# Summing the second layer's modulation vectors on VectorE instead of TensorE

## The chip, the cores and the metric

The kernel runs on one core of one Trainium2 chip. What counts is the device time of one execution in microseconds (us). The five engines of the core (PE = TensorE, DVE = VectorE, ACT = ScalarE, POOL = GpSimd, SP, which here only issues DMAs) each run their own list of instructions in order and wait for each other by semaphores.

## The reference, cut to what matters

The program is a transformer block with dilated attention, followed by two layers that are modulated by a conditioning vector. Everything is fp32. The part that the change touches is the modulation of the second layer (i = 1):

```python
def modulation(cvec, w, b):
    m = jax.nn.silu(cvec) @ w + b              # (1024,) @ (1024, 6144)
    return jnp.split(m[..., None, :], 6, axis=-1)

for i in range(2):
    sh1, sc1, g1, sh2, sc2, g2 = modulation(c, w_mod[i], b_mod[i])
    csh1, csc1, cg1, csh2, csc2, cg2 = modulation(c_ctx, w_mod[i], b_mod[i])
    h = x * (1.0 + sc1) + sh1
    hc = xc * (1.0 + csc1) + csh1
    ...                                        # mixer of the layer
    x = layer_norm(alpha * x + g1 * y)
    x = layer_norm(alpha * x + g2 * mlp(x * (1 + sc2) + sh2))   # mlp: relu(h @ w1)**2 @ w2
```

Each weight matrix w_mod[i] is 1024 x 6144 fp32, 25.2 MB, and it is read for two vectors (c and c_ctx). In the last layer the context stream needs only sh1 and sc1, so four of the six slices are needed for one vector alone.

## The kernel before, in words

The tokens are 256 of the stream and 256 of the context, in four tiles T of 128 tokens (T = 0, 1 context; T = 2, 3 stream). Large products are done in three fp32r products each: a weight tile of 128 x 1024 (`raw`, 512 KB) is loaded by SP, ScalarE rounds it to `whi` (line 134), VectorE makes the remainder `wlo` (line 135), and TensorE adds hi*hi, hi*lo and lo*hi (`mm3`, lines 158 to 160).

The first layer's MLP (`mlp`) runs over eight groups g of 512 hidden units. In each group the first product (w1) makes four hidden column tiles; ScalarE takes the relu (line 1002), VectorE squares (`f`, line 1003), ScalarE and VectorE split the result into `fx` (lines 110 and 111); then the second product (w2) is added to `y` by VectorE (lines 1012 and 1014). In g = 0 the w1 product is done in two parts, first for the context tokens, then for the stream, because the modulated input `hB` of the tiles comes one by one from `modulate`: TensorE transposes the normalised rows r (line 194), ScalarE applies scale and shift (`hf`, line 302), VectorE splits into `hBh` and `hBl` (lines 304 and 305). At the same time GpSimd computes the new residual streams (`new_resid`, lines 955 and 956: eight operations of 128 x 1024).

The second layer's modulation is computed during this MLP by three generators `quad` in the list `fillers`. Each covers 2048 columns; in 8 steps k it loads two pieces `mvraw` of 128 x 1024 (512 KB, three buffers, line 246) and multiplies them on TensorE by `cst_m[:, k, :]`, the two conditioning vectors padded to 32 columns (line 240): four products of 512 columns in fp32, one for each group of 32 output partitions, into the PSUM bank "O". The result is copied with the bias on VectorE (line 256), transposed into columns by `to_cols` (line 194 and 272), or written to DRAM for later row broadcasts. `fill(rate[0])` advances a generator by so many steps whenever a weight tile is requested (`w_a`, `w_b`); rate is 2 in the MLP.

The order on each engine is decided when the program is built, by a scheduler with a timeline model (`schedule_with_timeline_sim=True`), so code that is written later can stand earlier on its engine.

Of the kernel before, what the change touches and what calls it, by code (L numbers as in the profile page):

```python
# [10 lines left out]
F32 = mybir.dt.float32  # L11
# [3 lines left out]
ALU = mybir.AluOpType  # L15
# [80 lines left out]
def body(tc, a, cst, out):  # L96
    nc = tc.nc
    with ExitStack() as ctx:
        const = ctx.enter_context(tc.tile_pool(name="const", bufs=1))
        wpool = ctx.enter_context(tc.tile_pool(name="wpool", bufs=5))  # L100
        small = ctx.enter_context(tc.tile_pool(name="small", bufs=6))
        dram = ctx.enter_context(tc.tile_pool(name="dram", bufs=1, space=DRAM))
# [3 lines left out]
        def bank(tag):  # L106
            return psum.tile([P, 512], F32, tag=tag, name=tag, bufs={"mm": 3, "S": 2, "T": 2, "O": 1}[tag])
# [5 lines left out]
        fillers = []  # L113
# [12 lines left out]
        rate = [0]  # L126
# [81 lines left out]
        cst_m = const.tile([P, KC, 32], F32, tag="cst_m", name="cst_m")  # L208
        nc.gpsimd.memset(cst_a, 0.0)
        nc.gpsimd.memset(cst_m, 0.0)  # L210
        nc.gpsimd.memset(neghalf, -0.5)
        nc.vector.tensor_copy(cst_a[:, :, 0], cv[:, 2, :])
        make_identity(nc, ident)
        xs = const.tile([P, 2, D], F32, tag="xs", name="xs")
# [7 lines left out]
        b1 = ctx.enter_context(ExitStack())  # L222
        p1t = b1.enter_context(tc.tile_pool(name="p1t", bufs=2))

        def quad(pool, rpool, key, w, col, b, stat, vecs, n=512, rows=""):


            bias = pool.tile([P, n], F32, tag="mvb", name="mvb", bufs=1)
            nc.gpsimd.memset(bias, 0.0)
            for m in range(vecs):  # L230
                nc.gpsimd.dma_start(bias[m::32, :], b[col:col + 4 * n].rearrange("(j n) -> j n", n=n))
            acc = bank("O")
            wv = w.rearrange("(p k) n -> p k n", k=KC)
            todo = []

            def product():
                k, raws_ = todo.pop(0)
                for j in range(4):
                    raw = raws_[j * n // 1024]
                    nc.tensor.matmul(acc[32 * j:32 * j + 32, :n], stat[:, k, :], raw[:, j * n % 1024:j * n % 1024 + n], start=k == 0, stop=k == KC - 1)  # L240

            for k in range(KC):
                raws_ = []
                for h in range(n // 256):
                    raw = pool.tile([P, 1024], F32, tag="mvraw", name="mvraw", bufs=3)
                    nc.sync.dma_start(raw, wv[:, k, col + 1024 * h:col + 1024 * h + 1024])
                    raws_.append(raw)
                    yield
                todo.append((k, raws_))
                if len(todo) > 0:  # L250
                    product()
            while todo:
                product()
                yield
            r = rpool.tile([P, n], F32, tag="R" + key, name="R" + key, bufs=1) if rpool else tmp([P, n], "R" + key)
            nc.vector.tensor_add(r, acc[:, :n], bias)
            R[key] = r
            if rows:
                rd = dram.tile([vecs, 4 * n], F32, tag="rd" + rows, name="rd" + rows)
                for m in range(vecs):  # L260
                    nc.gpsimd.dma_start(rd[m].rearrange("(j n) -> j n", n=n), r[m::32, :])
                RD[rows] = rd
            yield

        def to_cols(r, name, tag="T"):

            pt = bank(tag)
            n = r.shape[-1] // P
            for c in range(n):
                transpose(pt[:, c * P:(c + 1) * P], r[:, c * P:(c + 1) * P])  # L270
            cols = const.tile([P, 4, n, 2], F32, tag=name, name=name)
            nc.vector.tensor_copy(cols, pt[:, :n * P].rearrange("p (c j r) -> p j c r", j=4, r=32)[:, :, :, 0:2])
            return cols.rearrange("p j c m -> p (j c) m")

        def to_rows(g, key, vec, at):

            nc.gpsimd.dma_start(g, bcast_rows(RD[key][vec, at:at + D]))
# [168 lines left out]
        def quad0():
            yield from quad(p1t, None, "0", w_mod[0], 0, b_mod[0], cst_m, 2)
            m0["a"] = to_cols(R["0"], "m0a")

        fillers.append(quad0())  # L450
        fillers.append(quad(p1t, const, "b", w_mod[0], 2048, b_mod[0], cst_m, 2, rows="b0"))
        fillers.append(quad(p1t, const, "c", w_mod[0], 4096, b_mod[0], cst_m, 2, rows="c0"))
        rate[0] = 2

        qT, kT = [], []
# [126 lines left out]

        fill(100)
        to_rows(gate, "g", 0, 0)
        m0a = m0["a"]
        m0b = to_cols(R["b"], "m0b")
        m0c = to_cols(R["c"], "m0c")

        alpha = 4.0 ** 0.25
        hH, hL = (slot(t, "h" + t, [P, KC, 512], F32R) for t in ("A0", "A1"))  # L590
# [373 lines left out]
        def mlp(layer, Ts, xks, y, pool, mid, norm, after):  # L964

            n = len(Ts) * P
            w1, w2 = a["mlp_w1_2"][layer], a["mlp_w2_2"][layer]
            for g in range(8):
                fx = (main, pool)[g % 2].tile([P, 8, n], F32R, tag=("qkb", "fx")[g % 2], name="fx")
                fh, fl = fx[:, 0:4], fx[:, 4:8]  # L970
                if layer and g < 1:
# [71 lines left out]

        lm = ctx.enter_context(ExitStack())
        pm = lm.enter_context(tc.tile_pool(name="pm", bufs=1, reuse_waits="tile"))
        m1a, m1b = {}, {}
        fillers.append(quad(pm, pm, "0", w_mod[1], 0, b_mod[1], cst_m, 2))
        fillers.append(quad(pm, const, "b", w_mod[1], 2048, b_mod[1], cst_m, 2, rows="b1"))
        fillers.append(quad(pm, const, "c", w_mod[1], 4096, b_mod[1], cst_m, 2, rows="c1"))
        lnr = ln_rows([pm.tile([P, D], F32, tag="lnr", name="lnr0", bufs=2) for _ in range(2)], (0, 0))  # L1050
        todo = [3]

# [6 lines left out]
                to_rows(gx, "c0", 0, D)  # L1059

        y0 = slot("A0", "y0", [P, 4, D])
        rate[0] = 2
        mod1 = {}

        def after0(T):
            if not mod1:
                fill(100)
                mod1["a"], mod1["b"], mod1["c"] = to_cols(R["0"], "m0a"), to_cols(R["b"], "m0b"), to_cols(R["c"], "m0c")
                ma = mod1["a"]
                mod1["h"] = new_h("hC")  # L1070
                mod1["cc"] = mod_cols("c0a", 3, 7, ma[:, 8:16], ma[:, 0:8], 1)
                mod1["cx"] = mod_cols("x0a", 3, 7, ma[:, 8:16], ma[:, 0:8], 0)
                mod1["ln"] = ln_rows([pm.tile([P, D], F32, tag="lnr", name="lnr1", bufs=2) for _ in range(2)], (0, 1))
            modulate(y0[:, T, :], (mod1["cc"], mod1["cx"])[T // 2], mod1["h"], P * T)
            if T > 1:
                new_resid(T, y0[:, T, :], mod1["ln"])
# [59 lines left out]
        for half, xk_ in ((1, hx), (0, hc)):  # L1136
# [13 lines left out]
            for e, nat, oth in sides:  # L1150
                for sl, src in ((nat, kT), (oth, kS)):
                    nc.scalar.copy(KK[sl, 0, :, e, hs], src[sl, :, hs])
                    nc.vector.tensor_sub(KK[sl, 1, :, e, hs], src[sl, :, hs], KK[sl, 0, :, e, hs].bitcast(F32))
        to_rows(gx, "b1", 0, 0)

        def window(kv, c, qt):

# [38 lines left out]
                    window(kv, c, qt)  # L1196

        r1 = slot("A0", "r1", [P, 4, D])
        m1c, m1b = mod1["c"], mod1["b"]
        cx = mod_cols("x0b", 4, 8, m1c[:, 0:8], m1b[:, 8:16], 0)  # L1200
        h2 = new_h("hD")
        mod2 = lambda T: modulate(r1[:, T, :], cx, h2, P * (T - 2))
        proj_out(r1, a["od_w_out_2"][0], aH, aL, (2, 3), mod2)
# [6 lines left out]
        for T in (2, 3):  # L1210
            new_resid(T, r1[:, T, :], lnr)
        lnr = ln_rows([pz.tile([P, D], F32, tag="lnr3", name="lnr3", bufs=2) for _ in range(2)], (1, 1))
        to_rows(gx, "c1", 0, D)
        y1 = slot("A0", "y1", [P, 4, D])

        done = []
# [39 lines left out]
```

## Time and profile before

| | us |
|---|---|
| median of 3 runs | 1420.35 (1417.97 to 1421.64) |
| profiled execution | 1420.52 |
| its span | 1418.7 |
| PE busy in the span | 1335.0 (94%) |
| DVE busy | 787.8 (56%) |
| ACT busy | 540.2 (38%) |
| POOL busy | 212.9 (15%) |
| first MLP: context part of g = 0 starts | about 652 |
| g = 1 starts / g = 7 starts | 707.4 / 1005.2 |

The profiled execution lies within the range of the three runs. Its own time is 1.8 us above its span. Busy shares are unions of instruction times; a matmul row shows 0.40 us, while the next one starts 0.23 us later, because matmuls are pipelined.

### The profile page before, as it was taken

To read this page: it belongs to the slowest core of one execution; us is meant where nothing else is said; L and a number is where in the kernel's file an instruction comes from. 1 tells how busy PE (TensorE), PEld (TensorE's weight loads), DVE (VectorE), ACT (ScalarE), POOL (GpSimd) and SP (SyncE) were. 2 spreads that over 40 slices of the span, in tenths; PEclk is the share of its full clock that TensorE was granted. 3 is DMA by queue.
4 is the path that set the end of the run, shared out by engine and by line. 5 is a ranking of instruction groups with operands and counts; after the bars stand their busy time and mean duration, and the time that the engine had idled before them with its cause. 6 is when DMAs were issued, how large, how long until landed. Compare 5 with 4: busy or idle time off the path is not lost.

```text
span 1418.7 us, 19881 instructions
## 1 busy us (share of the span) xinstructions
PE 1335.0 (94%) x7918; PEld 1056.4 (74%) x7918; DVE 787.8 (56%) x1254; ACT 540.2 (38%) x859; POOL 212.9 (15%) x196
## 2 busy tenths in 40 slices
PE   6999998999899999898999999999979799899995
PEld 5788865589787777676777767767859677698985
DVE  3544444345834358467444344434677966766667
ACT  2433434335531453223323223222335576454541
POOL 2110021000201200117000000000342644300001
PEclk9999999999999999899999999999989999899998
DMA  9988885565521411327643553553223503465651
GB/s 331 307 275 292 274 278 146 177 211 162 153 75 60 126 43 60 119 79 257 198 151 119 177 177 117 165 166 90 91 96 90 163 16 105 133 207 168 190 178 45
DMA packets 137987, 222.27 MB, mean 157 GB/s; under 512 B 8604, under 2 KB 86012, under 8 KB 137894
## 3 DMA queue, kind: packets, MB, share of 16 engines
q1 hardware_dynamic: 131984, 206.07, 45.7%
q0 software_dynamic: 5168, 14.38, 3.5%
q8 instruction: 62, 1.02, 0.3%
q10 hardware_dynamic: 742, 0.55, 0.1%
q14 instruction: 31, 0.25, 0.1%
HBM read 217.19 MB, written 1.16 MB: 154 GB/s over the span
## 4 chain that ended last, share of the span: by engine, by line
PE 84%; DVE 9%; DMA 2%; issue 2%; ACT 1%; POOL 0%; SPq 0%; DVEq 0%; ACTq 0%; POOLq 0%
PE mm L158 22%; PE mm L159 22%; PE mm L160 21%; PE O L240 5%; PE T L194 2%; DVE wlo L135 2%; PE mm L416 1%; PE O L1187 1%; PE S L1162 1%; PE S L523 1%; DMA mvraw<-in_w_mod_dram 1%; DMA raw<-in_w_in_dram 1%; PE T L748 1%; PE O L883 1%; PE O L546 1%
## 5 line engine op out<-in xcount | busy, mean ns | idle before, releaser
L135 DVE TENSOR_TENSOR wlo<-raw,whi 128x1024 fp32r<-128x1024 f32 x255 | 323.5, 1272 | 239.1 <-ACT whi L134 237.9
L134 ACT CAST whi<-raw 128x1024 fp32r<-128x1024 f32 x261 | 273.2, 1050 | 441.0 <-PE mm L160 251.9
L158 PE MATMUL mm<-whi,fx 128*128 128x512 f32 x384 | 155.4, 405 | 6.8 <-DVE tm L935 3.3
L159 PE MATMUL mm<-wlo,fx 128*128 128x512 f32 x384 | 151.9, 396 | 0.0
L160 PE MATMUL mm<-whi,fx 128*128 128x512 f32 x384 | 145.5, 397 | 0.0
L158 PEld LDWEIGHTS mm<-whi,fx 128*128 128x128 f32 x384 | 72.4, 188 | 42.9 <-DVE y L1014 11.9
L158 PE MATMUL mm<-A1a,whi 128*128 128x256 f32 x352 | 101.0, 287 | 0.0
L160 PE MATMUL mm<-A1a,wlo 128*128 128x256 f32 x352 | 100.0, 284 | 0.0
L159 PE MATMUL mm<-A1a,whi 128*128 128x256 f32 x352 | 100.0, 284 | 0.0
L159 PE MATMUL mm<-hBl,whi 128*128 128x512 f32 (+1 forms) x256 | 97.6, 382 | 1.0 <-DVE v L327 0.7
L1014 DVE TENSOR_TENSOR y<-y,mm 128x512 f32<-128x512 f32 x72 | 47.3, 683 | 70.7 <-PE mm L160 70.1
L160 PEld LDWEIGHTS mm<-whi,fx 128*128 128x128 f32 x384 | 72.5, 189 | 18.7 <-DVE f L1003 0.8
L159 PEld LDWEIGHTS mm<-wlo,fx 128*128 128x128 f32 x384 | 72.6, 189 | 15.4
L240 PE MATMUL O<-mvraw,cst_m 128*32 128x512 f32 x384 | 76.3, 608 | 7.2 <-DMA mvraw<-in_w_mod_dram 7.2
L158 PEld LDWEIGHTS mm<-A1a,whi 128*128 128x128 f32 x352 | 66.3, 188 | 12.9 <-issue 11.1
L159 PEld LDWEIGHTS mm<-A1a,whi 128*128 128x128 f32 x352 | 66.3, 188 | 6.1 <-issue 6.0
L160 PEld LDWEIGHTS mm<-A1a,wlo 128*128 128x128 f32 x352 | 66.3, 188 | 3.1 <-issue 2.8
L159 PE MATMUL mm<-hDl,whi 128*128 128x256 f32 x224 | 63.0, 281 | 0.0
L159 PEld LDWEIGHTS mm<-hBl,whi 128*128 128x128 f32 x256 | 48.2, 188 | 12.3 <-DVE hBl L305 2.3
L1003 DVE TENSOR_TENSOR f<-f,mm 128x512 f32<-128x512 f32 (+1 forms) x58 | 32.1, 555 | 44.8 <-ACT f L1002 44.6
L1002 ACT ACTIVATE f<-mm 128x512 f32<-128x512 f32 (+1 forms) x58 | 28.5, 491 | 71.3 <-PE mm L160 70.3
L158 PE MATMUL mm<-whi,hA 128*128 128x512 f32 x128 | 51.3, 401 | 0.0
(481 smaller groups left out, 2928.1 us busy)
## 6 DMA issues: line engine op xcount, KB each, us to landing
raw<-in_mlp_w_dram SPq DMA_DIRECT2D x128, 512.0 KB, 4.1
mvraw<-in_w_mod_dram SPq DMA_DIRECT2D x96, 512.0 KB, 4.6
raw<-in_w_in_dram SPq DMA_DIRECT2D x64, 512.0 KB, 6.7
raw<-in_ev_w_in_dram SPq DMA_DIRECT2D x25, 512.0 KB, 4.7
raw<-in_od_w_qkv_dram SPq DMA_DIRECT2D x12, 512.0 KB, 3.5
mvraw<-in_w_ada_dram SPq DMA_DIRECT2D x10, 512.0 KB, 6.7
raw<-in_w_out_dram SPq DMA_DIRECT2D x8, 512.0 KB, 3.7
raw<-in_ev_w_out_dram SPq DMA_DIRECT2D x8, 512.0 KB, 3.8
```

The source lines that it names most:

```text
L134: nc.scalar.copy(hi, raw)
L135: (nc.gpsimd if weng and weng.pop() else nc.vector).tensor_sub(lo, raw, hi.bitcast(F32))
L158: nc.tensor.matmul(o, lh, rh, start=first, stop=False)
L159: nc.tensor.matmul(o, lh, rl, start=False, stop=False)
L160: nc.tensor.matmul(o, ll, rh, start=False, stop=last)
L194: nc.tensor.transpose(o, i, ident[:n, :n])
L240: nc.tensor.matmul(acc[32 * j:32 * j + 32, :n], stat[:, k, :], raw[:, j * n % 1024:j * n % 1024 + n], start=k == 0, stop=k == KC - 1)
L416: nc.tensor.matmul(o[:, j, :], w_[:, k, js], h_[:, 2 * p + k, :], start=(p, j, k, n) == (0, 0, 0, 0), stop=(p, k, n) == (3, 1, 2), skip_gr ...
L523: nc.tensor.matmul(sv[e][:, g - g0, :], qT[g][sl, h2, qt * P:(qt + 1) * P], kT[g][sl, h2, 0:nk], start=True, stop=True)
L1002: nc.scalar.activation(f, o, AF.Relu)
L1003: nc.vector.tensor_mul(f, f, o)
L1014: nc.vector.tensor_add(y[:, T, hs], y[:, T, hs], o)
```

## The change

A new generator `summed` computes one slice of 1024 columns for one or two vectors. For each k VectorE multiplies the piece `raw` by a scalar for each partition (`stat[:, k, m]`, the vector's element that belongs to this partition and k) and adds it to an accumulator `acc` of 128 x 1024 (`scalar_tensor_tensor`, fp32; for k = 0 a `tensor_scalar_mul`). After eight steps TensorE adds up the 128 partitions with `sel`, a matrix with ones in one column, in four products of 256 columns for each vector. The bias is added on VectorE, and the slice is transposed to columns or written to DRAM. There are six slices, two for two vectors and four for one: 64 accumulating operations on VectorE (8 of them with k = 0) and 32 products on TensorE take the place of 96 products of 512 columns. The pieces of weight that are loaded are the same 48, with the same three buffers. The rate is 0 in g = 0 and 2 from g = 1 on. In the first layer the three quads stay, and their `to_cols` is called by the generator itself.

```diff
+        sel = const.tile([P, 2, 32], F32, tag="sel", name="sel")
+        nc.gpsimd.memset(sel, 0.0)
+        for m in range(2):
+            nc.gpsimd.memset(sel[:, m, m:m + 1], 1.0)
...
+        def summed(pool, res, key, w, col, b, stat, vecs, rows=False):
+            n = D // 4
+            r = pool.tile([P, n], F32, tag="mvb", name="mvb", bufs=1)
+            nc.gpsimd.memset(r, 0.0)
+            for m in range(vecs):
+                nc.gpsimd.dma_start(r[m::32, :], b[col:col + D].rearrange("(j n) -> j n", n=n))
+            accs = [pool.tile([P, D], F32, tag="mva", name="mva", bufs=2) for _ in range(vecs)]
+            wv = w.rearrange("(p k) n -> p k n", k=KC)
+            for k in range(KC):
+                raw = pool.tile([P, D], F32, tag="mvraw", name="mvraw", bufs=3)
+                nc.sync.dma_start(raw, wv[:, k, col:col + D])
+                yield
+                for m, acc in enumerate(accs):
+                    if k:
+                        nc.vector.scalar_tensor_tensor(acc, raw, stat[:, k, m:m + 1], acc, op0=ALU.mult, op1=ALU.add)
+                    else:
+                        nc.vector.tensor_scalar_mul(acc, raw, stat[:, k, m:m + 1])
+            o = bank("O")
+            for m, acc in enumerate(accs):
+                for j in range(4):
+                    nc.tensor.matmul(o[32 * j:32 * j + 32, :n], sel[:, m, :], acc[:, n * j:n * j + n], start=m == 0, stop=m == vecs - 1)
+            nc.vector.tensor_add(r, o[:, :n], r)
...
+                res[key] = to_cols(r, key, "O")
...
             for g in range(8):
+                if g == 1:
+                    rate[0] = 2
...
-        fillers.append(quad(pm, pm, "0", w_mod[1], 0, b_mod[1], cst_m, 2))
-        fillers.append(quad(pm, const, "b", w_mod[1], 2048, b_mod[1], cst_m, 2, rows="b1"))
-        fillers.append(quad(pm, const, "c", w_mod[1], 4096, b_mod[1], cst_m, 2, rows="c1"))
+        mod1 = {}
+        for i, key in enumerate(("sh1", "sc1", "ga1", "sh2", "sc2", "ga2")):
+            fillers.append(summed(pm, mod1, key, w_mod[1], D * i, b_mod[1], cst_m, 2 if i < 2 else 1, i % 3 == 2))
...
-        rate[0] = 2
-        mod1 = {}
+        rate[0] = 0
```

Where the new operations stand is the scheduler's doing. On VectorE at the start of the MLP, before the change, between the subtraction for `hBl` of tile 2 and the end of the splitting of the last tile (T = 3; r is its normalisation, hBh and hBl its split):

```order
L327 TENSOR_SCALAR v<-mvst 128x1
L305 TENSOR_TENSOR hBl<-hf,hBh_5265 128x4x128
L304 CAST hBh0b<-hf 128x4x128
L305 TENSOR_TENSOR hBl<-hf,hBh0b 128x4x128
L333 TENSOR_SCALAR r_5254<-r_5254,mvst,rs_y 128x1024
L304 CAST hBh_5265<-hf 128x4x128
```

The same place now (the new lines are 285 and 287; the lines after them have moved, 370 is the normalisation, 341 and 342 the split):

```order
L285 SCALAR_TENSOR_TENSOR mva<-mvraw,cst_m,mva 128x1024
L364 TENSOR_SCALAR v<-mvst 128x1
L342 TENSOR_TENSOR hBl<-hf,hBh0b 128x4x128
L285 SCALAR_TENSOR_TENSOR mva<-mvraw,cst_m,mva 128x1024 x5
L370 TENSOR_SCALAR r_5258<-r_5258,mvst,rs_y 128x1024
L285 SCALAR_TENSOR_TENSOR mva<-mvraw,cst_m,mva 128x1024 x5
L341 CAST hBh_5269<-hf 128x4x128
L341 CAST hBh0b<-hf 128x4x128
L287 TENSOR_SCALAR mva<-mvraw,cst_m 128x1024
L342 TENSOR_TENSOR hBl<-hf,hBh_5269 128x4x128
```

Although the rate is 0 in g = 0, all sixteen accumulating operations of the first slice (sh1) stand ahead of the last tile's split: two with k = 0 and three more stand just above the rows shown. Of the 64 operations the order has 16 ahead of that split's end, 24 in the rest of g = 0, 20 in g = 1 and 4 in g = 2.

On TensorE, where the stream's part of g = 0 begins, before:

```order
L159 MATMUL S<-hBl,whi 128x256
L160 MATMUL S<-hBh0b,wlo 128x256
L240 MATMUL O<-mvraw,cst_m 32x512 x6
L158 MATMUL mm<-hBh_5265,whi 128x256 x2
L158 MATMUL S<-hBh_5265,whi 128x256 x2
L159 MATMUL mm<-hBl,whi 128x256
```

And now, with line 291 for the selecting products:

```order
L160 MATMUL S<-hBh0b,wlo 128x256
L194 MATMUL T<-ident,r_5258 128x128 x8
L291 MATMUL O<-mva,sel 32x256 x8
L158 MATMUL mm<-hBh_5269,whi 128x256 x2
L158 MATMUL S<-hBh_5269,whi 128x256 x2
L159 MATMUL mm<-hBl,whi 128x256
```

The products with `mvraw` are gone, and the eight selecting products of the first slice and the transposes of T = 3 stand directly in front of the stream's part, so that part is queued behind the first slice's last accumulation on VectorE.

## Rows read from the trace of the kernel before

**Rows 1.** Page, part 1: busy us (share of the span) x instructions.
```profile
PE 1335.0 (94%) x7918; PEld 1056.4 (74%) x7918; DVE 787.8 (56%) x1254; ACT 540.2 (38%) x859; POOL 212.9 (15%) x196
```
**Rows 2.** Windows from:to, length, busy us of each engine, granted clock, DMA share, GB/s.
```profile
640.00:700.00 60.00, 52.96 (x326) 39.84 (x327) 39.11 (x40) 20.32 (x40) 25.02 (x14) 0.94 0.70 243
700.00:960.00 260.00, 260.00 (x1141) 191.43 (x1140) 107.26 (x135) 67.45 (x82) 4.42 (x8) 1.00 0.47 150
```
**Rows 3.** Chain of waits by line, 707.3 to 990 us.
```profile
by line: PE mm L158 31.2%; PE mm L159 30.0%; PE mm L160 29.9%; PE O L240 8.5%; PE T L194 0.5%
```
**Rows 4.** Windows for line 240 alone: PE busy, PEld busy, clock, DMA share, GB/s.
```profile
707.30:990.00 282.70, 25.41 (x140) 4.17 (x140) 1.00 0.46 146
```
**Rows 5.** Timeline of PE around one step: start us, us, engine, line, instruction.
```profile
833.54 0.39 PE L160 MATMUL mm<-whi,fx 128*128 128x512 f32 x1
833.86 1.07 PE L240 MATMUL O<-mvraw,cst_m 128*32 128x512 f32 x8
834.86 0.51 PE L158 MATMUL mm<-whi,fx 128*128 128x512 f32 x1
```
**Rows 6.** Timeline of PE, the first block's products of 256 columns with 32.
```profile
78.04 1.07 PE L240 MATMUL O<-mvraw,cst_a 128*32 128x256 f32 x16
79.04 0.39 PE L158 MATMUL mm<-A1a,whi 128*128 128x256 f32 x1
```
**Rows 7.** Timeline of DVE at the start of the MLP.
```profile
637.18 0.83 DVE L333 TENSOR_SCALAR r<-r,mvst,rs_y 128x1024 f32<-128x1024 f32 x1
638.53 0.42 DVE L304 CAST hBh0b<-hf 128x512 fp32r<-128x512 f32 x1
641.93 2.35 DVE L135 TENSOR_TENSOR wlo<-raw,whi 128x1024 fp32r<-128x1024 f32 x2
644.81 1.96 DVE L304 CAST hBh<-hf 128x512 fp32r<-128x512 f32 x1
656.80 2.90 DVE L333 TENSOR_SCALAR r<-r,mvst,rs_y 128x1024 f32<-128x1024 f32 x1
664.75 2.29 DVE L304 CAST hBh<-hf 128x512 fp32r<-128x512 f32 x1 [5.05 <-ACT hf L302]
```
**Rows 8.** Timeline of POOL in the same stretch: first and last of eight operations.
```profile
643.40 5.57 POOL L955 TENSOR_TENSOR A1t<-r,lnr 128x1024 f32<-128x1024 f32 x2 [1.75 <-DMA lnr<-in_ln_g_dram]
664.38 2.38 POOL L956 TENSOR_TENSOR xs<-xs,lnr 128x1024 f32<-128x1024 f32 x1
```
**Rows 9.** Timeline of DVE and POOL at the end of the MLP.
```profile
1000.41 1.22 DVE L1018 SCALAR_TENSOR_TENSOR y<-A1t,y 128x1024 f32<-128x1024 f32 x1
1003.92 3.42 DVE L1018 SCALAR_TENSOR_TENSOR y<-A1t,y 128x1024 f32<-128x1024 f32 x1 [0.64 <-POOL y L1017]
1000.57 5.68 POOL L1017 TENSOR_TENSOR y<-y,A1t 128x1024 f32<-128x1024 f32 x2 [0.39 <-DVE y L1014]
```
**Rows 10.** Timeline of PE: the parts of g = 0, and g = 1.
```profile
652.08 0.39 PE L159 MATMUL mm<-hBl,whi 128*128 128x256 f32 x1 [0.25 <-DVE hBl L305]
667.10 0.51 PE L158 MATMUL mm<-hBh,whi 128*128 128x256 f32 x2
707.39 0.39 PE L158 MATMUL mm<-hBh,whi 128*128 128x512 f32 x1
```
**Rows 11.** DMAs of mvraw, 600 to 1010 us.
```profile
DMA to landing us min/median/max: 3.5/4.6/10.3
```
**Rows 12.** Windows (columns as rows 2) in which TensorE has nothing, then works again.
```profile
644.00:646.00 2.00, 0.00 (x0) 0.00 (x0) 2.00 (x3) 1.36 (x4) 2.00 (x1) 0.50 0.97 315
650.00:652.00 2.00, 1.83 (x9) 0.79 (x8) 2.00 (x2) 1.50 (x4) 2.00 (x2) 0.88 1.05 408
```
**Rows 13.** Window of g = 1 (columns as rows 2).
```profile
707.30:757.00 49.70, 49.70 (x223) 37.29 (x222) 21.74 (x33) 13.06 (x16) 1.67 (x3) 1.00 0.47 149
```
**Rows 14.** DVE by group, 667 to 707.3 us: busy us, mean ns | idle before, releaser.
```profile
L135 DVE TENSOR_TENSOR wlo<-raw,whi 128x1024 fp32r<-128x1024 f32 x7 | 8.6, 1223 | 9.9 <-ACT whi L134 9.9
L111 DVE TENSOR_TENSOR fx<-f,fx 128x512 fp32r<-128x512 f32 x4 | 2.7, 687 | 0.2
```

More of the change, by code (lines that the diff above doesn't have):

```diff
@@ L262, in quad @@
                 RD[rows] = rd
+            yield
[10 more added lines that the diff above has]
+                nc.sync.dma_start(raw, wv[:, k, col:col + D])
+                yield
+                for m, acc in enumerate(accs):
[8 more added lines that the diff above has]
+            nc.vector.tensor_add(r, o[:, :n], r)
+            if rows:
+                rd = dram.tile([vecs, D], F32, tag="rd" + key, name="rd" + key)
+                for m in range(vecs):
+                    nc.gpsimd.dma_start(rd[m].rearrange("(j n) -> j n", n=n), r[m::32, :])
+                RD[key] = rd
+            else:
+                res[key] = to_cols(r, key, "O")
             yield
@@ L444, in body, with quadcols @@
         m0 = {}
[L446 to L452, printed above, removed]
+        def quadcols(key, col, rows=""):
+            yield from quad(p1t, None, key, w_mod[0], col, b_mod[0], cst_m, 2, rows=rows)
+            m0[key] = to_cols(R[key], "m0" + key)
+        fillers.append(quadcols("0", 0))
+        fillers.append(quadcols("b", 2048, "b0"))
+        fillers.append(quadcols("c", 4096, "c0"))
         rate[0] = 2
@@ L584, in body @@
         to_rows(gate, "g", 0, 0)
-        m0a = m0["a"]
-        m0b = to_cols(R["b"], "m0b")
-        m0c = to_cols(R["c"], "m0c")
+        m0a, m0b, m0c = m0["0"], m0["b"], m0["c"]
         alpha = 4.0 ** 0.25
@@ L1045, in body @@
         pm = lm.enter_context(tc.tile_pool(name="pm", bufs=1, reuse_waits="tile"))
-        m1a, m1b = {}, {}
-        fillers.append(quad(pm, pm, "0", w_mod[1], 0, b_mod[1], cst_m, 2))
-        fillers.append(quad(pm, const, "b", w_mod[1], 2048, b_mod[1], cst_m, 2, rows="b1"))
-        fillers.append(quad(pm, const, "c", w_mod[1], 4096, b_mod[1], cst_m, 2, rows="c1"))
+        mod1 = {}
+        for i, key in enumerate(("sh1", "sc1", "ga1", "sh2", "sc2", "ga2")):
+            fillers.append(summed(pm, mod1, key, w_mod[1], D * i, b_mod[1], cst_m, 2 if i < 2 else 1, i % 3 == 2))
         lnr = ln_rows([pm.tile([P, D], F32, tag="lnr", name="lnr0", bufs=2) for _ in range(2)], (0, 0))
@@ L1061, in body @@
         y0 = slot("A0", "y0", [P, 4, D])
-        rate[0] = 2
-        mod1 = {}
+        rate[0] = 0
         def after0(T):
-            if not mod1:
+            if "h" not in mod1:
                 fill(100)
-                mod1["a"], mod1["b"], mod1["c"] = to_cols(R["0"], "m0a"), to_cols(R["b"], "m0b"), to_cols(R["c"], "m0c")
-                ma = mod1["a"]
                 mod1["h"] = new_h("hC")
-                mod1["cc"] = mod_cols("c0a", 3, 7, ma[:, 8:16], ma[:, 0:8], 1)
-                mod1["cx"] = mod_cols("x0a", 3, 7, ma[:, 8:16], ma[:, 0:8], 0)
+                mod1["cc"] = mod_cols("c0a", 3, 7, mod1["sc1"], mod1["sh1"], 1)
+                mod1["cx"] = mod_cols("x0a", 3, 7, mod1["sc1"], mod1["sh1"], 0)
                 mod1["ln"] = ln_rows([pm.tile([P, D], F32, tag="lnr", name="lnr1", bufs=2) for _ in range(2)], (0, 1))
@@ L1153, in body @@
                     nc.vector.tensor_sub(KK[sl, 1, :, e, hs], src[sl, :, hs], KK[sl, 0, :, e, hs].bitcast(F32))
-        to_rows(gx, "b1", 0, 0)
+        to_rows(gx, "ga1", 0, 0)
         def window(kv, c, qt):
@@ L1198, in body @@
         r1 = slot("A0", "r1", [P, 4, D])
-        m1c, m1b = mod1["c"], mod1["b"]
-        cx = mod_cols("x0b", 4, 8, m1c[:, 0:8], m1b[:, 8:16], 0)
+        cx = mod_cols("x0b", 4, 8, mod1["sc2"], mod1["sh2"], 0)
         h2 = new_h("hD")
@@ L1212, in body @@
         lnr = ln_rows([pz.tile([P, D], F32, tag="lnr3", name="lnr3", bufs=2) for _ in range(2)], (1, 1))
-        to_rows(gx, "c1", 0, D)
+        to_rows(gx, "ga2", 0, 0)
         y1 = slot("A0", "y1", [P, 4, D])
```

## The prediction, made before the changed kernel was run

> **What bounds the kernel now.** I read the page's table first: TensorE is busy 94% of the span, VectorE 56% [rows 1]. That is an average, so I then read windows by stage. From 700 to 960 us, in the first MLP, TensorE has no gap at all (260 of 260 us) and VectorE works 107 of 260, 41% [rows 2]. At the start of the MLP, 640 to 700, it is another picture: TensorE works 53 of 60 us, VectorE 39, GpSimd 25, and the granted clock is 0.94. So the change takes work from TensorE where it is the bound, and gives it to VectorE, which has room from g = 1 on, but not at the start of g = 0. The chain of waits from 707.3 to 990 us says what TensorE's part is worth: line 240 holds 8.5% of 282.7 us, 24.0 us [rows 3]; its busy time there is 25.4 us [rows 4]. The timeline shows the same for one step: the matmuls around it start 1.32 us apart instead of 0.23, so a step of four products of 512 columns costs 1.09 us [rows 5].
>
> **Which part of the gain counts.** A step is eight instructions, two for each product [rows 5], so the second layer's 96 products are 192. Of these 140 come after 707.4, where g = 1 starts [rows 4, 10]; the other 52 are in g = 0, 24 of them ahead of its stream part at 667, where TensorE waits for tiles anyway. After 707.4 I count 25.4 us as saved. What comes in there: 16 of the 32 selecting products, four groups of four. A group of four with 256 columns costs 0.5 us (two groups, 16 instructions, hold TensorE from 78.04 to 79.04) [rows 6], so 2.0 us. Of the 12 transposes to columns (1.4 us, 0.5% of the chain [rows 3]) four are left, 0.9 us less. Gain after 707.4: 25.4 - 2.0 + 0.9 = 24.3 us.
>
> **What the start costs.** The price of an accumulating operation on 128 x 1024 is that of the scalar_tensor_tensor with two SBUF inputs at the MLP's end, 1.22 us [rows 9]; that of the operation with k = 0 is a normalisation's, 0.83 us [rows 7]. In the order, all sixteen of the first slice stand ahead of the last tile's split, and TensorE's stream part is queued behind that split and behind the slice's selecting products. So I follow VectorE from 644.28, the end of two casts' remainders [rows 7], to the stream's part, which starts at 667.1 before [rows 10]:
> - New work: 14 x 1.22 + 2 x 0.83 = 18.7 us.
> - Idle time that it fills: 5.05 us, in which VectorE waited for ScalarE's hf [rows 7].
> - Waiting for GpSimd: VectorE's casts and normalisations take 1.96 to 2.90 us there in place of 0.42 and 0.83 [rows 7]. They are six, the first at 644.81 and the last at 664.75, and together they are 11.9 us over their price. GpSimd runs eight operations of 128 x 1024 from 643.40 on, of 2.38 us where nothing is in the way [rows 8], and VectorE's operation ends each time just after one of them. The new operations are of the kind that waits too: the same scalar_tensor_tensor took 3.42 us when it met GpSimd's operation [rows 9]. Now VectorE has such an operation queued at nearly every moment of GpSimd's eight: 8 x 2.38 = 19.0, less 0.9 already run at 644.28 and 0.6 beside a statistics operation, makes 17.5 us of waiting, 5.6 more than before.
> - The eight selecting products (1.0 us) and the next slice's first operation (0.83) stand between the sixteenth accumulation and the end of the split; half of the first overlaps: 1.4 us.
>
> Sum: 18.7 - 5.05 + 5.6 + 1.4 = 20.6 us later. The loads keep up: three buffers, a landing of 4.6 us [rows 11] and two operations of 1.22 make (4.6 + 2.4) / 3 = 2.3 us for each piece, VectorE's own pace; at the slowest landing, 10.3 us, it is 4.2, and the five pieces behind the first three cost 9 us more.
>
> The Trainium skill (page "SBUF — State Buffer", section "SBUF: two separate sides") says that VectorE and GpSimd share a pair of SBUF ports by an exclusive lock: a VectorE operation with two SBUF inputs and a GpSimd operation that reads SBUF never run side by side, the loser blocks for the whole instruction. Rows 9 agree (3.42 us against 1.22). By this rule the term stays at 5.6 us; if the two only shared the ports' bandwidth, it would go, and the sum below would be 1418.
>
> Next, the stream's part and the first w2. Up to its last fx VectorE has 11 accumulations and one with k = 0 (14.2 us), four remainders of 1.22 (4.9), eight operations of 0.69 (5.5) [rows 14] and small ones, 25 us. TensorE then has 69 of the 96 products of w2 to do (three banks are open, and only the fourth k waits), 69 x 0.23 = 15.9, with 1.0 for the second slice's selecting products and 1.6 in which they wait for its last three accumulations (3.7 us, against nine matmuls, 2.1). That is 43.5 us against the 40.3 from 667.1 to 707.4 [rows 10]: 3.2 more. Loss at the start of g = 1: 20.6 + 3.2 = 23.8 us.
>
> Bounds of this loss: below, 12 us, if the waiting on GpSimd doesn't grow, the stream part's accumulations are hidden, and tile 2's transposes, which stood behind products with mvraw, bring 3 us. Above, 33 us, with the slow landing.
>
> **What else moves.** VectorE in g = 1 has 21.7 us of old work [rows 13], and the order adds 20 accumulations, 17 x 1.22 + 3 x 0.83 = 23.2: 44.9 us, where TensorE needs 96 x 2 x 0.23 = 44.2 and 1.0 for selecting. It will be late here and there: I take 2 us, from 0 (its work all fits between the waits) to 9 (two fifths of the new 23.2 us not hidden). From g = 2 on only four operations are left, and TensorE has its full gain. TensorE idles longer at the start: in such a gap its granted clock was 0.50, and 0.88 in the window in which it took up work again [rows 12], that is, the lower of its two levels (1.2 GHz) for some microseconds; the products are then twice as long, and with VectorE the later one most of it is hidden: 1.5 us, bounds 0 and 4. The first layer's transposes stand earlier, with the same instructions: 0, bounds -1 and 1. GpSimd's bias loads and the two row writes stand in a queue that works 4.4 of 260 us after 700 [rows 2]: 0; if they were late, the slice's sum on VectorE would wait, which is in the upper bound of the 2 us.
>
> Sum, against the profiled execution's 1420.5 us: + 23.8 - 24.3 + 1.5 + 2 = + 3.0, 1423.5. That execution lies at the median of the three runs (1420.35), so I forecast 1424.
>
> **The rivals.** A result is told from no change when it is over 0.3%, 4.3 us, away.
> - My forecast, the loss at the start eats the gain: 1424, its own range 1416 to 1431. For it speak the order and the durations; against it, that both terms are 24 us and of one size by chance.
> - The start hides it, faster: the loss is at its lower bound, 12, nothing is late in g = 1, and the gain of 24.3 comes through: 1420.5 + 12 - 24.3 = 1408. For it: TensorE has 7 us without work from 640 to 700 already [rows 2], and its products with mvraw waited for their loads there. Against: the sixteen operations stand on the very engine that sets this stretch.
> - VectorE stays the later engine through g = 0 and g = 1, and TensorE stops at each group of selecting products until the slice's last accumulation is done: 1420.5 + 33 - 24.3 + 9 = 1438. It decides once VectorE's work of a group is over TensorE's 45 us. For it: 44.9 us against 45; against: 41% of use before [rows 2], and only one such group.
>
> That the work leaves TensorE is sure from the order (96 products of 512 columns become 32 of 256), so I give no chance to a change without effect on TensorE.
>
> **How the numbers follow.** Forecast 0.52: by its range, slower 0.24, same 0.24, faster 0.04. Hidden start 0.24: faster 0.20, same 0.04. VectorE late throughout 0.24: slower 0.22, same 0.02. Together faster 0.24, same 0.30, slower 0.46. The range, 1409 to 1438, goes from next to the second case to the third and leaves a tenth out at either end.
>
> **What would show it.** Right: in the new profile the stream's part of g = 0 starts near 688 instead of 667, g = 1 near 731, the accumulations between 644 and 685 take up to 3.5 us while GpSimd runs, the stage from g = 2 to 960 us has no line of products but the MLP's own, and each g from the third on takes about 45 us instead of 49.5. Wrong: if the stream's part starts before 680, the second case holds; if TensorE's waits name the accumulators at line 291 in g = 1 for over 5 us, the third.

## The result, and the profile after

The changed kernel takes 1432.72 us (median of 4 runs, 1429.98 to 1434.82); the kernel before, on the same chip, 1420.8 (4 runs). The ratio is 1.0079, 95% interval 1.0061 to 1.0097: slower, by 0.8%. The forecast was 1424, with a range of 1409 to 1438. The sum that led to it was + 3.0 us; measured are + 11.9. The execution profiled after took 1429.98 us with a span of 1428.2, 9.5 more than the span before.

The page of the changed kernel, engines and the new accumulations, answers to [rows 1]:

```profile
PE 1315.2 (92%) x7786; PEld 1060.5 (74%) x7786; DVE 859.3 (60%) x1322; ACT 539.9 (38%) x859; POOL 219.1 (15%) x202
...
L285 DVE SCALAR_TENSOR_TENSOR mva<-mvraw,cst_m,mva 128x1024 f32<-128x1024 f32 x56 | 72.7, 1314 | 8.9 <-DMA mvraw<-in_w_mod_dram 8.9
```

TensorE has 20 us less to do and VectorE 72 more. An accumulation is 1.31 us in the mean, 1.27 where nothing is in its way. The windows that answer to [rows 2] (from:to, length, busy of PE, PEld, DVE, ACT, POOL, granted clock, DMA share, GB/s), and those of four groups g of the changed kernel:

```profile
640.00:700.00 60.00, 33.04 (x206) 29.18 (x205) 54.31 (x54) 16.20 (x37) 33.05 (x18) 0.72 0.58 185
700.00:960.00 260.00, 252.39 (x1136) 199.34 (x1135) 165.11 (x199) 74.48 (x94) 6.03 (x13) 1.00 0.51 162
...
737.74:785.48 47.74, 46.64 (x211) 36.40 (x210) 39.64 (x45) 12.89 (x16) 2.28 (x5) 1.00 0.85 277
785.48:832.31 46.83, 46.74 (x207) 36.44 (x206) 30.43 (x39) 12.57 (x16) 0.86 (x2) 1.00 0.52 170
832.31:878.30 45.99, 45.67 (x197) 36.11 (x196) 20.53 (x26) 13.06 (x16) 0.56 (x1) 1.00 0.30 92
878.30:923.62 45.32, 45.01 (x193) 36.01 (x192) 20.09 (x25) 13.08 (x16) 0.00 (x0) 1.00 0.31 93
```

At the start VectorE is now the busy one (54 of 60 us, 39 before) and TensorE stands for 27 us. Later TensorE's groups shrink to 45.3 us; before, the six groups from 707.39 to 1005.18 took 49.6 in the mean. The marks of the timeline of PE: the first transposes of the MLP (T = 0), the end of g = 0's context part, the selecting products, the stream part, g = 1 and g = 7, to hold against [rows 10]:

```profile
642.59 1.03 PE L194 MATMUL T<-ident,r 128*128 128x128 f32 x8
670.53 0.58 PE L159 MATMUL mm<-hBl,whi 128*128 128x256 f32 x1 [6.75 <-DVE hBl L342]
686.62 0.64 PE L291 MATMUL O<-mva,sel 128*32 128x256 f32 x8 [2.07 <-DVE mva L285]
693.99 0.58 PE L159 MATMUL mm<-hBl,whi 128*128 128x256 f32 x1 [4.55 <-DVE hBl L342]
737.74 0.40 PE L158 MATMUL mm<-hBh,whi 128*128 128x512 f32 x1
...
1014.25 0.40 PE L158 MATMUL mm<-hBh,whi 128*128 128x512 f32 x1
```

The first transposes in the kernel before:

```profile
634.65 1.03 PE L194 MATMUL T<-ident,r 128*128 128x128 f32 x8
```

So the whole MLP begins 7.9 us later, the stream part 26.9, g = 1 30.35; g = 7 comes at 1014.25 in place of 1005.18, 9.07 later. Taken apart: + 7.9 ahead of the MLP, + 19.0 in its start, + 3.5 up to g = 1, - 21.3 in the six groups after that, + 0.4 behind g = 7: + 9.5. The prediction had the first layer, which lies ahead of the MLP, at 0 us.

The 7.9 us begin in the first block. The timeline there, kernel before: the attention's score transposes (T<-ident,pr), its bias loads (B), the first layer's sum (Rb):

```profile
185.39 0.55 PE L194 MATMUL T<-ident,pr 128*128 128x128 f32 x3
192.95 0.82 POOL L510 DMA_DIRECT2D B<-tabd  x1 [7.24 <-DVE m L526]
222.67 0.69 DVE L256 TENSOR_TENSOR Rb<-O,mvb 128x512 f32<-128x512 f32 x1 [0.50 <-PE O L240]
```

The same in the changed kernel:

```profile
213.43 0.69 DVE L260 TENSOR_TENSOR Rb<-O,mvb 128x512 f32<-128x512 f32 x1 [3.26 <-PE O L244]
214.18 1.11 PE L194 MATMUL T<-ident,Rb 128*128 128x128 f32 x4 [0.80 <-DVE Rb L260]
214.41 1.14 POOL L265 DMA_DIRECT2D rdb<-Rb  x2 [29.84 <-DVE Rb L260]
215.08 1.49 PE L194 MATMUL T<-ident,pr 128*128 128x128 f32 x6
218.77 1.86 POOL L547 DMA_DIRECT2D B<-tabd  x2 [1.27 <-DVE m L563]
```

The attention's first score transposes come 30 us later, right behind those of Rb, and GpSimd waits 29.84 us for Rb with six bias loads behind the row write. TensorE has other work meanwhile (products with mvraw), so the 30 us do not all count: VectorE's operation on zp, a step behind the attention that stood at 261.76 us, comes 11.3 us later, the MLP 7.9. From 210 to 230 us TensorE is busy 17.2 of 20 us instead of 19.2, at a granted clock of 0.74 instead of 1.00 (windows, kernel before and then the changed one):

```profile
210.00:230.00 20.00, 19.20 (x127) 11.79 (x127) 8.80 (x23) 7.56 (x15) 4.63 (x7) 1.00 0.81 243
```

```profile
210.00:230.00 20.00, 17.22 (x82) 10.70 (x79) 8.50 (x28) 6.90 (x16) 4.64 (x7) 0.74 0.59 186
```

Two things follow it in the changed order, GpSimd's wait and TensorE's transposes; the experiments had to tell which one leads.

### The profile page after: what moved, and what is told of

Read it like the earlier page. It is cut to its first block, busy times and chain, and to the rows that moved or that the text cites. A ratio compares the mean times of both kernels' runs of the same rounds, so it can differ in the third digit from the quotient of the medians.

```text
span 1428.2 us, 19747 instructions
## 1 busy us (share of the span) xinstructions
PE 1315.2 (92%) x7786; PEld 1060.5 (74%) x7786; DVE 859.3 (60%) x1322; ACT 539.9 (38%) x859; POOL 219.1 (15%) x202
## 4 chain that ended last, share of the span: by engine, by line
PE 77%; DVE 12%; issue 5%; DMA 4%; ACT 1%; POOL 0%; SPq 0%; DVEq 0%; ACTq 0%; POOLq 0%
PE mm L158 21%; PE mm L159 20%; PE mm L160 20%; PE O L244 3%; DMA mvraw<-in_w_mod_dram 3%; DVE mva L285 2%; DVE wlo L135 2%; PE T L194 2%; PE mm L453 1%; PE O L1220 1%; PE S L1195 1%; DMA B<-tabd 1%; PE O L422 1%; DVE y L1051 1%; PE T L783 1%
## 5 line engine op out<-in xcount | busy, mean ns | idle before, releaser
L159 PE MATMUL mm<-hBl,whi 128*128 128x512 f32 (+1 forms) x256 | 99.5, 390 | 11.3 <-DVE hBl L342 11.3
L285 DVE SCALAR_TENSOR_TENSOR mva<-mvraw,cst_m,mva 128x1024 f32<-128x1024 f32 x56 | 72.7, 1314 | 8.9 <-DMA mvraw<-in_w_mod_dram 8.9
L159 PEld LDWEIGHTS mm<-hBl,whi 128*128 128x128 f32 x256 | 50.1, 196 | 22.1 <-DVE hBl L342 11.9
L1054 POOL TENSOR_TENSOR y<-y,A1t 128x1024 f32<-128x1024 f32 x6 | 18.0, 3015 | 307.6 <-DVE y L1051 307.6
L158 PE MATMUL mm<-hBh,whi 128*128 128x512 f32 (+1 forms) x128 | 50.5, 398 | 9.6 <-DVE hBh L341 9.6
L110 ACT CAST fx<-f 128x512 fp32r<-128x512 f32 (+1 forms) x60 | 31.1, 520 | 67.9 <-DVE f L1040 67.9
```

The lines of the kernel that those rows point to most:

```text
L110: nc.scalar.copy(hi, src)
L158: nc.tensor.matmul(o, lh, rh, start=first, stop=False)
L159: nc.tensor.matmul(o, lh, rl, start=False, stop=False)
L285: nc.vector.scalar_tensor_tensor(acc, raw, stat[:, k, m:m + 1], acc, op0=ALU.mult, op1=ALU.add)
L1054: nc.gpsimd.tensor_mul(y[:, T, :], y[:, T, :], (gc, gx)[T // 2])
```

## The experiments

The table holds, for each profiled execution, the start of the MLP's first transposes, the time from there to the first product of w2 (the "front"), and from there to g = 7; the ratios are against the kernel before of the same batch (1420.8 to 1421.5 us). Kernels that share the old first block differ by up to 5 us in the first column (633.0 to 637.9), and the profiled executions of e2 and e3 were 4.6 and 5.7 us above their medians, that of e5 4.0 below its own. So a few us between two single profiles decide nothing; the timed ratios do.

| | us | ratio, 95% | transposes | front | to g = 7 |
|---|---|---|---|---|---|
| before | 1420.8 | | 634.7 | 44.2 | 370.5 |
| after | 1432.7 | 1.0079 (1.0061 to 1.0097) | 642.6 | 64.7 | 371.7 |
| e1 second layer only | 1424.5 | 1.0026 (1.0014 to 1.0038) | 637.9 | 65.2 | 372.5 |
| e2 first layer only | 1429.0 | 1.0061 (1.0039 to 1.0082) | 648.0 | 44.2 | 371.2 |
| e3 rows on SyncE | 1429.5 | 1.0057 (1.0035 to 1.0079) | 647.2 | 65.1 | 373.6 |
| e5 no wait on GpSimd | 1427.9 | 1.0038 (1.0024 to 1.0052) | 638.9 | 64.4 | 371.3 |
| e9 columns in bank O | 1425.2 | 1.0033 (1.0020 to 1.0045) | 637.4 | 65.0 | 371.9 |
| e4 sums after g = 0 | 1397.4 | 0.9832 (0.9810 to 0.9854) | 633.0 | 45.8 | 346.5 |
| e10 bank O and late sums | 1398.2 | 0.9843 (0.9822 to 0.9863) | 636.1 | 44.7 | 345.2 |
| e6 narrow sums | 1401.4 | 0.9859 (0.9837 to 0.9881) | 634.9 | 51.1 | 350.7 |
| e7 no residual | 1403.0 | 0.9865 (0.9844 to 0.9885) | 635.7 | 46.9 | 348.7 |
| e8 before, no residual | 1422.5 | 1.0007 (0.9994 to 1.0021) | 634.0 | 41.6 | 372.7 |

**Second layer alone, first layer alone (e1, e2).** The edit of e1 takes back the first layer's part (cut, against the changed kernel); e2 is the kernel before with that part alone:

```diff
-        fillers.append(quadcols("0", 0))
-        fillers.append(quadcols("b", 2048, "b0"))
-        fillers.append(quadcols("c", 4096, "c0"))
...
+        fillers.append(quad0())
+        fillers.append(quad(p1t, p1t, "b", w_mod[0], 2048, b_mod[0], cst_m, 2, rows="b0"))
+        fillers.append(quad(p1t, p1t, "c", w_mod[0], 4096, b_mod[0], cst_m, 2, rows="c0"))
...
-        m0a, m0b, m0c = m0["0"], m0["b"], m0["c"]
+        m0a = m0["a"]
+        m0b = to_cols(R["b"], "m0b")
+        m0c = to_cols(R["c"], "m0c")
```

The generator `quad0` makes the columns of slice "0" itself, as in the kernel before. The results of b and c lie in the pool p1t here, where the kernel before had them in const; the rest is undone.

> The changed kernel with its edits to the first layer undone: the modulation of the first layer is turned into columns as in the kernel before, behind the attention, and the second layer is summed on VectorE as in the change. In the trace after the change the MLP starts 8 us later than before. Theory A: these 8 us come from the first layer's edits, which put the write of its rows ahead of six loads of the attention's bias in GpSimd's queue: the MLP's first transposes return to about 635 us, the MLP itself is as after the change, and the time is about 1424.5 (1432.7 - 8). Rival B: the 8 us come from the second layer's edits (the new tiles, other buffers, other loads): the time stays at about 1432.

> The kernel before with only the first layer's edits. Theory A: the first layer's edits alone cost the 8 us ahead of the MLP: the MLP's first transposes come at about 642.5 us as after the change, and the time is about 1428.5 (1420.8 + 8). Rival B: they cost nothing by themselves: about 1421.

Both times came out by theory A: 1424.5 and 1429.0. (The first transposes of e2 came at 648.0 and not near 642.5, in an execution 4.6 us above its median.) The first layer's edits alone cost 7.9 us, the second layer's 3.4; together 11.3, and 11.9 were measured. e1 is what the prediction had summed.

**What of the first layer costs it (e3, e5, e9).** e3 sends the row write by SyncE; e5 in addition gives `mvb`, the bias tile of the sums, two buffers (one of three such lines is shown); e9 leaves both as in the change and only names another bank:

```diff
-                    nc.gpsimd.dma_start(rd[m].rearrange("(j n) -> j n", n=n), r[m::32, :])
+                    nc.sync.dma_start(rd[m].rearrange("(j n) -> j n", n=n), r[m::32, :])
```
```diff
-            bias = pool.tile([P, n], F32, tag="mvb", name="mvb", bufs=1)
+            bias = pool.tile([P, n], F32, tag="mvb", name="mvb", bufs=(2 if pool is p1t else 1))
```
```diff
-            m0[key] = to_cols(R[key], "m0" + key)
+            m0[key] = to_cols(R[key], "m0" + key, "O")
```

> The changed kernel with one edit: the write of the first layer's rows is issued by SyncE's queue and not by GpSimd's, so that the loads of the attention's bias no longer stand behind it. All arithmetic of the first layer stays where the change put it. Theory A (the queue): the bias loads are issued near 194 us again instead of 218.8, most of the 8 us come back, and the time is about 1425. Rival B (TensorE's transposes of the first layer, which now stand among the attention's products and wait for VectorE, cost the time): it stays at about 1432.

> The changed kernel with the first layer's row writes on SyncE's queue and a second buffer for the bias tile mvb, so that neither the row write nor the filling of the next bias tile, which waits for the same Rb, stands ahead of the attention's bias loads in GpSimd's queue (with the row writes alone moved, the trace showed GpSimd waiting 29.12 us for Rb in front of the memset of mvb instead). The first layer's transposes stay where the change put them. Theory A (the queue of GpSimd costs the first layer's 8 us): the bias loads are issued near 194 us as in the kernel before, not at 218, the MLP's first transposes come near 635, and the time is about 1424.5, that of the second layer alone. Rival B (the transposes among the attention's products, or their wait for VectorE, cost it): the loads are early and the time stays between 1429 and 1432.

> The changed kernel with one word more: the first layer's columns are transposed into the PSUM bank O and not into one of the two banks T. All that GpSimd, SyncE and VectorE do for them stays. The run without GpSimd's wait for Rb showed the bias loads still late (216.03 us), now behind the attention's own score reduction (m, 31.97 us of waiting), so the queue of GpSimd is a follower and not the cause. Theory C (the two T banks are given out in the program's order: the tile for Rb's transposes is held until Rb is there, at 213 us, and the attention's transposes of its scores, which take the T tiles after it, wait behind it): the first attention's score transposes come near 185 us again, the bias loads near 194, the MLP's first transposes near 635, and the time is about 1424.5. Rival B (transposes among the attention's products cost it wherever they land, now in the single bank O that the attention's second product also needs): 1429 to 1433.

e3 (1429.5) tells nothing apart: GpSimd then waited 29.12 us in front of the filling of mvb, which needs the same Rb. In e5 that wait is gone, and still the bias loads are late. Timeline of e5:

```profile
211.98 0.69 DVE L260 TENSOR_TENSOR Rb<-O,mvb 128x512 f32<-128x512 f32 x1 [2.34 <-PE O L244]
212.73 0.66 PE L194 MATMUL T<-ident,Rb 128*128 128x128 f32 x4 [0.80 <-DVE Rb L260]
213.22 0.99 PE L194 MATMUL T<-ident,pr 128*128 128x128 f32 x6
216.03 1.86 POOL L547 DMA_DIRECT2D B<-tabd  x2 [31.97 <-DVE m L563]
```

The loads wait for the attention's own score reduction now (31.97 <-DVE m), and the attention's transposes still follow those of Rb. My first theory, GpSimd's queue, falls as the leading cause. With the columns in bank O (e9) everything is back at its old place, though not one instruction was taken away. Timeline of e9:

```profile
184.91 0.55 PE L194 MATMUL T<-ident,pr 128*128 128x128 f32 x3
192.47 0.82 POOL L547 DMA_DIRECT2D B<-tabd  x1 [7.24 <-DVE m L563]
222.96 0.69 DVE L260 TENSOR_TENSOR Rb<-O,mvb 128x512 f32<-128x512 f32 x1 [0.50 <-PE O L244]
223.94 1.19 POOL L265 DMA_DIRECT2D rdb<-Rb  x2 [0.43 <-DVE Rb L260]
```

1425.2 against the expected 1424.5: the cause lies in bank T. `to_cols` asks for one of its two tiles ahead of the attention and needs it until Rb is there, and in the order that the scheduler built, the attention's transposes, which ask behind it, all follow those of Rb. Why the second tile did not serve the first of them, the runs don't show. (The first layer's result also moved to another buffer in the change; e9 leaves that as it is, so it is not the cause.) e5 came back part of the way (1427.9; its interval lies below that of the change, and overlaps e2's and e3's), so GpSimd's wait may cost a few us of its own; this stays open.

**When the sums run (e4, e10).** `st1` is a copy of the conditioning vectors that hangs on the last tile of g = 0, so no accumulation can be placed ahead of it. e4 has the old first layer, e10 that of e9:

```diff
+                    if not layer:
+                        nc.vector.scalar_tensor_tensor(st1, y[:, 3, 0:2 * KC].rearrange("p (k m) -> p k m", m=2), 0.0, cst_m[:, :, 0:2], op0=ALU.mult, op1=ALU.add)
...
-            fillers.append(summed(pm, mod1, key, w_mod[1], D * i, b_mod[1], cst_m, 2 if i < 2 else 1, i % 3 == 2))
+            fillers.append(summed(pm, mod1, key, w_mod[1], D * i, b_mod[1], st1, 2 if i < 2 else 1, i % 3 == 2))
```

> The second layer's sum as in the change, the first layer as before, and the accumulations made dependent on the last result of the MLP's first group, so that none can stand ahead of it on VectorE. Theory A (the accumulations on VectorE set the start of the MLP's stream part, 18 us of the loss, and 4 us of the first group's end): this loss goes, the gain of 21 us by the last group stays except for what the late sums cost in the second group, and the time is about 1402 to 1406. Rival B (the start waits for the weights' loads or for GpSimd's residual and not for the accumulations): it gains under 5 us on the run with the second layer alone, so 1420 to 1425.

> The whole change, mended in both places: the first layer's columns in bank O, and the second layer's accumulations dependent on the last result of the MLP's first group. If the two losses are independent of each other, it is as fast as the second layer alone with late sums, 1395 to 1400 (1397.35 there); if the first layer's columns cost something wherever they stand, 1402 to 1408.

Windows of e4: the front, and g = 1:

```profile
632.98:678.73 45.75, 36.09 (x239) 33.54 (x238) 35.45 (x37) 19.98 (x44) 27.39 (x18) 0.85 0.46 155
701.73:749.49 47.76, 46.42 (x211) 36.40 (x210) 46.03 (x50) 12.79 (x16) 1.46 (x3) 1.00 0.69 216
```

The front is back at 45.8 us with VectorE busy 35 of them, and g = 1, where VectorE is busy 46.0 of 47.8 us, is no longer than in the changed kernel (47.74). The time, 1397.35, is below the 1402 to 1406 of theory A, since the part of g = 0 with w2 shrinks too: 701.73 - 678.73 = 23.0 us, 28.55 before, when 28 instructions of line 240 stood in it (5.29 us). e10 has the whole change with both places mended, and its time is that of e4 within the intervals: nothing is left of the first layer's loss, and the two losses are independent. Both are 1.6 to 1.7% faster than the kernel before.

**What makes the front long (e6, e7, e8).**

The first edit is e6's, the second that of e7 and e8:

```diff
-                        nc.vector.scalar_tensor_tensor(acc, raw, stat[:, k, m:m + 1], acc, op0=ALU.mult, op1=ALU.add)
+                        nc.vector.scalar_tensor_tensor(acc[:, 0:32], raw[:, 0:32], stat[:, k, m:m + 1], acc[:, 0:32], op0=ALU.mult, op1=ALU.add)
```
```diff
-                for T in range(4):
-                    new_resid(T, r0[:, T, :], lnr)
```

> The second layer alone, with each accumulation on 32 of the 1024 columns (the rest of the sum is left out); the loads, the first product of each tile and TensorE's products with the selector stay. Theory A (the accumulations' time on VectorE sets the start of the MLP): from the first transposes to the first product of w2 it is 44 to 49 us (66.9 with the second layer alone, 44.2 in the kernel before), the gain by the last group stays, and the time is 1397 to 1403. Rival B (the loads of the modulation's weights ahead of the MLP's own on SyncE's queue set it): the 66.9 stay above 60, and the time is 1415 to 1424.

> The second layer alone, without the new residual that GpSimd and VectorE make at the start of the MLP (the normalised old row times gain plus offset is left out, the sum goes on with what the tiles held). Theory A (part of the start's loss is VectorE waiting for its port while GpSimd works on that residual): no accumulation takes over 2 us (3.35 beside GpSimd, 1.28 alone), and the stretch from the first transposes to the first product of w2 is 6 to 17 us shorter than 66.9, more than in the same cut of the kernel before. Rival B (the accumulations' own time is all of it): the stretch shortens by no more than the same cut shortens that of the kernel before.

> The kernel before with the same residual left out, to compare e7 with. Theory A: the 44.2 us from the first transposes to the first product of w2 shorten by less than in e7, by 0 to 12 us. Rival B: by as much as in e7 or more.

(The 66.9 us of these expectations are 65.2 by the first product of w2 at 703.08.) e6: with little of the sums left (the operations with k = 0 stay whole) the front is 51.1 us, 14 shorter, but 7 above the old one, so neither figure holds exactly; the loads, which all stay, are not the bulk of it. Even these short operations wait for GpSimd; four, and six, take 2.89 and 5.39 us, where a single one takes 0.24. Timeline of e6, VectorE and then GpSimd:

```profile
660.28 0.23 DVE L285 SCALAR_TENSOR_TENSOR mva<-mvraw,cst_m,mva 128x32 f32<-128x32 f32 x1
661.10 2.89 DVE L285 SCALAR_TENSOR_TENSOR mva<-mvraw,cst_m,mva 128x32 f32<-128x32 f32 x4
664.64 5.39 DVE L285 SCALAR_TENSOR_TENSOR mva<-mvraw,cst_m,mva 128x32 f32<-128x32 f32 x6
...
661.58 2.36 POOL L993 TENSOR_TENSOR xs<-xs,lnr 128x1024 f32<-128x1024 f32 x1
664.80 2.38 POOL L992 TENSOR_TENSOR xs<-r,lnr 128x1024 f32<-128x1024 f32 x1 [0.86 <-DVE r L370]
667.26 2.39 POOL L993 TENSOR_TENSOR xs<-xs,lnr 128x1024 f32<-128x1024 f32 x1
```

e7 tells most. Without the residual the front falls from 65.2 to 46.9 us, by 18.3, more than the 6 to 17 expected, no accumulation takes over 2 us, and the time falls by 21.6 (the ratio by 1.6%); the same cut in the kernel before shortens the front by 2.6 us and the time not at all. Accumulations and residual each fit into the start, both together don't. The accumulations in the front, by group, e1 and then e7:

```profile
L285 DVE SCALAR_TENSOR_TENSOR mva<-mvraw,cst_m,mva 128x1024 f32<-128x1024 f32 x20 | 26.8, 1377 | 0.0
L287 DVE TENSOR_SCALAR mva<-mvraw,cst_m 128x1024 f32<-128x1024 f32 x4 | 7.1, 1790 | 4.7 <-DMA mvraw<-in_w_mod_dram 4.7
```

```profile
L285 DVE SCALAR_TENSOR_TENSOR mva<-mvraw,cst_m,mva 128x1024 f32<-128x1024 f32 x14 | 17.5, 1279 | 0.0
L287 DVE TENSOR_SCALAR mva<-mvraw,cst_m 128x1024 f32<-128x1024 f32 x2 | 1.4, 750 | 3.9 <-DMA mvraw<-in_w_mod_dram 3.9
```

33.9 us become 18.9: 9.2 of the 15.0 are eight operations that no longer stand ahead of w2 (6 x 1.28 + 2 x 0.75); the other 5.8 are waiting. How much of the 18.3 us is waiting and how much the other order that the scheduler chose, this cut can't part.

## Why the prediction was right and wrong

**The step that failed** is the term "The first layer's transposes stand earlier, with the same instructions: 0, bounds -1 and 1." The instructions are the same, but they ask for a T tile ahead of the attention, and the attention's transposes stand behind them. Measured: 7.9 us in the profile, 8.2 between the medians of the change and e1, 7.9 as e2 alone, gone in e9 by a change of bank. No row of that stretch was read. The rest of the sum, + 3.0, meets e1 (+ 3.4, by the ratio + 2.0 to + 5.4).

That the time lies within 1409 to 1438 is luck in part. The upper end came from the case in which VectorE is late throughout, which did not happen; by the forecast's own range, 1416 to 1431, 1432.7 is too long. And the second layer alone (e1, + 0.26%) would have been no change by the prediction's measure of 0.3%: the term that stood at 0 makes the result slower.

**The loss at the start.** Forecast 20.6, measured 19.0 (41.79 - 22.82); the windows of VectorE's stretch, kernel before and changed:

```profile
644.28:667.10 22.82, 18.86 (x129) 14.30 (x129) 17.70 (x15) 5.48 (x16) 21.71 (x10) 0.86 0.55 205
```

```profile
652.20:693.99 41.79, 18.22 (x128) 16.09 (x126) 38.22 (x34) 5.23 (x15) 27.98 (x11) 0.66 0.56 181
```

Two of its terms were off in opposite directions, and that they nearly cancel is luck too. "Idle time that it fills: 5.05": 3.57 us of idle remain (41.79 - 38.22), now in front of the first load of mvraw, so 1.5 are filled. "5.6 more than before" of waiting for GpSimd: rows of the changed kernel say otherwise.

```profile
655.80 4.22 DVE L287 TENSOR_SCALAR mva<-mvraw,cst_m 128x1024 f32<-128x1024 f32 x2 [3.57 <-DMA mvraw<-in_w_mod_dram]
660.55 1.96 DVE L341 CAST hBh<-hf 128x512 fp32r<-128x512 f32 x1
662.43 2.57 DVE L341 CAST hBh0b<-hf 128x512 fp32r<-128x512 f32 x1
664.92 3.35 DVE L285 SCALAR_TENSOR_TENSOR mva<-mvraw,cst_m,mva 128x1024 f32<-128x1024 f32 x1
668.53 1.27 DVE L285 SCALAR_TENSOR_TENSOR mva<-mvraw,cst_m,mva 128x1024 f32<-128x1024 f32 x1
...
681.71 6.05 DVE L285 SCALAR_TENSOR_TENSOR mva<-mvraw,cst_m,mva 128x1024 f32<-128x1024 f32 x5
681.86 8.78 POOL L990 TENSOR_TENSOR xs<-r,lnr 128x1024 f32<-128x1024 f32 x1 [6.37 <-DVE r L370]
688.36 2.84 DVE L287 TENSOR_SCALAR mva<-mvraw,cst_m 128x1024 f32<-128x1024 f32 x1
691.12 2.82 DVE L342 TENSOR_TENSOR hBl<-hf,hBh 128x512 fp32r<-128x512 f32 x1
```

Over the prices alone (0.74, 0.41, 1.22, 0.68) these rows hold 12.8 us of waiting, against 11.9 before (of whose six operations one is a subtraction for hBl): + 0.9. From 681.86 on GpSimd waits as well: it needs 8.78 us for an operation of 2.38. With the third operation of k = 0 in the new work (14 x 1.22 + 3 x 0.74 = 19.3) the terms read 19.3 - 1.5 + 0.9 = 18.7; the selecting products at 686.62 are hidden behind the split that follows. The Trainium skill (page "SBUF — State Buffer", section "SBUF: two separate sides") gives the shared ports to whoever starts first, for the whole instruction; 3.35 us beside GpSimd against 1.27 alone agree. I had let VectorE lose each time, and the trace shows both sides losing.

**The first w2 and the gain.** For the stretch up to g = 1 the forecast had + 3.2, and 1.5 for the lower clock; + 3.5 are measured for both together, so the 1.5 is not seen apart. (In the profile after, the granted clock was 0.50, the level of 1.2 GHz, from 694 to 698 us, behind four us in which TensorE was busy for 0.01, and 1.00 from 702 on.) Less the 7.9 us, the stream part starts at 686.1 and g = 1 at 729.8, near the 688 and 731 that the prediction named as signs. Gain from g = 1 on, after lateness: 24.3 - 2 = 22.3 forecast, 21.3 measured; the first three groups are 2.4, 1.5 and 0.7 us longer than the 45.3 of the rest. The third case's sign, waits of TensorE for the accumulators at line 291 in g = 1 of over 5 us, did not show; no selecting product waits there, and TensorE stands only 0.51 and 0.59 us right behind two groups of them (765.58 for f, 771.19 for y). So the time lies nearer to the third case (1438) than to mine, but not by its mechanism.

**The "hidden start" case** (1408) was wrong for the order as built. With the sums behind g = 0 (e4) the start loses nearly nothing and the gain comes through: 1397.

## What to carry to other kernels

Work moved to an engine with room must be kept out of the stage where that engine is late: here a dependency that holds the sums back until g = 0 is done turned + 3.4 us into - 23.8. And a small step that is called earlier asks for its tile earlier: where a buffer has only two copies, the work that asks later can end up behind it, as the attention did here, however short the step is. So read the stretch around every moved allocation, not only its instructions.

## What the runs showed of the hardware that was not expected

While VectorE issued five accumulations of 1024 columns back to back, GpSimd's operation got no turn between them (681.86, 8.78 us; e1, e3 and e9 show the same within 0.02 us, e5 7.26). With accumulations of 32 columns it got its turn at once: e6 has it done in 2.36 to 2.39 us, and there VectorE's operations wait. Single VectorE operations of the changed kernel's start waited up to 2.16 us, no longer than one operation of GpSimd takes (2.38).

In the 20 us from 210 to 230 TensorE's granted clock was 0.74 in the mean in the changed kernel and 0.57 in e2, where the same stretch had 1.00 before. In the changed kernel it stood at 0.91 in the mean from 210 to 215, where TensorE was busy for 2.59 of the 5 us, and then at 0.50, the level of 1.2 GHz, although TensorE was busy again:

```profile
210.00:215.00 5.00, 2.59 (x12) 0.97 (x9) 0.86 (x2) 0.00 (x0) 0.59 (x1) 0.91 1.00 337
215.00:220.00 5.00, 4.85 (x22) 3.59 (x21) 2.92 (x11) 2.45 (x5) 3.43 (x7) 0.50 0.65 246
```

The transposes of Rb took 0.42 us each there; those of the slice before, at 166 us, took 0.27 each. So the delay has two parts, the gap and the slower work behind it; no run parts them.
